# Forgetting attention: the division by the softmax sums moved from the probabilities to the outputs

## The chip, the core and the metric

The kernel runs on one core of a Trainium2 chip. The core has a matrix engine (TensorE, PE in the profile; PEld is its loading of weights), three engines for elementwise work (VectorE or DVE, ScalarE or ACT, GpSimd or POOL), and a queue engine (SyncE, SP) that issues nearly all transfers between memory and the core. Results of TensorE land in eight PSUM banks. The metric is the device time of one execution in microseconds (us); lower is better.

## The reference, cut to what matters

One layer of a streaming encoder on 1024 tokens of width 1024, in float32. A normed input is projected; the columns go to three mixers side by side, whose outputs are joined, projected by `w_o` and added to x; then comes a gated feed-forward part and a last norm. The change lies in the third mixer, forgetting attention, with 8 heads of 64 columns:

```python
s = jnp.einsum('bhqd,bhkd->bhqk', qb, kh) + Fb[..., None] - F[:, :, None, :]
s = jnp.where(kpos[None, :] <= qpos[:, None], s, -jnp.inf)
p = jax.nn.softmax(s, axis=-1)
return jnp.einsum('bhqk,bhkd->bhqd', p, vh)
```

`softmax` divides every row of exponentials by its sum. The division may be done on the exponentials, or after the product with v on the outputs, one divisor for each query and head.

## The kernel before, in words

**Precision.** Every float32 operand of a matmul is split into a high part in a rounded type and the low rest. A product takes three matmuls (high by high, high by low, low by high), in `gemm` (L144) and `woven` (L152).

**Attention.** The 8 heads are worked on as 4 pairs `p` of 2 heads `a` (`fox_attend`, L627). For each head there are four items `m` of two query blocks of 128 (`fox_item`, L549), 32 items in all. An item forms the negated scores `s` of each query block (L575 to L578), adds F and takes the row's minimum on VectorE (L580), and takes the exponential on ScalarE, which also gives the row's sum as a column of `l` (L584). L587 takes reciprocals, and the probabilities are divided in place: the first block by GpSimd (L590), the second by VectorE (L592). Then, in steps of two key blocks, TensorE transposes the probabilities into a bank `pt` (L601), ScalarE and VectorE write the high and low part `pp` (L603, L604), and TensorE multiplies by `v` into the bank `o` (L615). At the end ScalarE copies the lower half of `o` (L618) and VectorE adds the two halves (L621). `o` and `Y` have 64 head columns on the partitions and queries along the free dimension. For pairs 0 to 2 the result is written into a tile `y0` to `y2`, and `keep_mix` (L270) splits it and stores it in memory (`mixs`, L275 and L276). For pair 3 each item writes its part of `last_mix` itself (L624, L625), and that stays on the core.

**What is threaded between.** While pair `p` is worked on, the projections of pair `p+1` (`fox_qk`, L532, tiles `zq`, `zk`; its results are `q`, `k`, `kl`) and, in pairs 0 and 1, of the second half of the values (`fox_values`, `psv`) are on TensorE too. During pairs 2 and 3 it is the output projection. `out_proj` (L651) is called twice for each of the 8 token blocks `tb`: first as `pxa` over the first four groups of mixer columns (L698 to L707), then as `pxb` over the last four. Each call has two groups of 12 matmuls, for two halves of the columns; each group fills a bank of the tag "gm", and L658 adds the bank to the tile `xa` of this token block, which L704 has loaded with x. The tag "gm" has two banks (`BANKS`, L27). `pxb` needs `last_mix` and the weights `wo4` to `wo7`.

**Slots.** Large tiles live in 33 slots of 128 partitions by 1024 elements. A list `idle` of slots is kept while the program is written out:

```python
i = idle.pop(0)                                              # L51, G: take a slot
t_ = big.tile([P, 1024], dtype, tag=f"g{i}", name=name)      # L52
idle.append(where.pop(n))                                    # L58, free: give it back at the end
```

A tile's slot is thus settled by the order in which the program calls `G` and `free`, and the first instruction that writes a tile waits for the last one that uses the tile that had its slot before. Behind pair 2 the program frees the slots of the normed input `hT` (16), of pair 2's `q`, `k`, `kl` and of `v2`, then those of `mh6` and `y2` by `keep_mix`. It then takes, in this order: `mix7` twice, weights `wo0` to `wo3` (two slots each), four mixes, `xa0` to `xa3`, four mixes, `xa4` to `xa7`, and, after giving back the mixes, the weights and pair 3's operands, `wo4` to `wo7`. Other tiles live in rings of a few slots (`RINGS`, L28); the ring `wr`, two slots, holds weights as they come from memory.

**Order.** Each engine works through its own list of instructions in order. These lists are made before the run by a planner (L1119) that follows a simulated time line: an instruction that is ready goes first if it stands earlier in the program, and later work fills the time in which earlier work waits.

Of the kernel before, what the change touches and what calls it, by code (L numbers as in the profile page):

```python
# [9 lines left out]
F32 = mybir.dt.float32  # L10
F32R = mybir.dt.float32r
I8 = mybir.dt.int8
AF = mybir.ActivationFunctionType
ALU = mybir.AluOpType
# [4 lines left out]
P = 128  # L19
# [12 lines left out]
def tile_hybrid_block(ctx: ExitStack, tc, x, w_fv, w_gv, w_zt, w_o, w_gu, w_down, ln, w_pool, w_a3, chans, b_f, consts, out):  # L32
    nc = tc.nc
    ACT, DVE, POOL, PE, SP = nc.scalar, nc.vector, nc.gpsimd, nc.tensor, nc.sync
# [4 lines left out]
    dpool = ctx.enter_context(tc.tile_pool(name="dp", bufs=1, space=bass.MemoryType.DRAM))  # L39
# [10 lines left out]
    def G(name, dtype=F32):  # L50
        i = idle.pop(0)  # L51
        t_ = big.tile([P, 1024], dtype, tag=f"g{i}", name=name)  # L52
        where[name] = i
        return t_

    def free(*names):
        for n in names:
            idle.append(where.pop(n))  # L58

    def R(name, dtype=F32, tag="p"):  # L60

        i = rings[tag].pop(0)
        rings[tag].append(i)
        return big.tile([P, 1024], dtype, tag=f"g{i}", name=name)

    def S(name, cols=1, dtype=F32):
        return sml.tile([P, cols], dtype, tag=f"s{cols}", name=name)

    def f(ap):
        return ap.bitcast(F32)  # L70


    ident = cst.tile([P, P], F32, name="ident")
# [38 lines left out]
    def PS(tag, name):  # L112
        return pst.tile([P, 512], F32, tag=tag, name=name, bufs=BANKS[tag])
# [22 lines left out]
    def half(name, dtype=F32):  # L136
        return rng.tile([P, 512], dtype, tag="tmp", name=name, bufs=2)
# [25 lines left out]
    def names_T(name):  # L163
        return [f"{name}{k}_{c}_{h}" for k in range(4) for c in range(2) for h in range(2)]
# [105 lines left out]
    def keep_mix(k, y):  # L270

        hi = G(f"mh{k}", F32R)
        ACT.activation(hi, y, AF.Copy)
        DVE.tensor_tensor(out=y, in0=y, in1=f(hi), op=ALU.subtract)
        SP.dma_start(mixs[k, :, 0], f(hi))  # L275
        SP.dma_start(mixs[k, :, 1], y)  # L276
        free(f"mh{k}")
# [14 lines left out]
    last_mix = []  # L292
# [253 lines left out]
                    POOL.tensor_copy(t_[a][own[1 - a], csl], f(t_[a][own[a], csl]))  # L546
        return Q, K, KL

    def fox_item(p, a, m, ops, fb, V, Y):  # L549

        Q, K, KL = (t_[a] for t_ in ops)
        nm = f"{p}_{a}_{m}"
        rows = slice(64 * a, 64 * a + 64)
        Pb, Ws = [], []
        l, rl = S(f"l{nm}", 2), S(f"rl{nm}", 2)
        for i in range(2):
            qb = 2 * m + i
            W = P * (qb + 1)
            nh = 1 if W <= 512 else 2
            w = W // nh  # L560
            qs = slice(qb * P, (qb + 1) * P)
            mn = S(f"mn{nm}_{i}")
            if m >= 2:
                pb = R(f"pb{nm}_{i}")
            elif i == 0:
                pb2 = R(f"pb{nm}")
                pb = pb2[:, 0:512]
            else:
                pb = pb2[:, 512:1024]
            top = 3.0e38  # L570
            for h in range(nh):
                s = PS("s", f"s{nm}_{i}_{h}")
                ks = slice(h * w, (h + 1) * w)
                last = h == nh - 1
                PE.matmul(s[:, 0:w], Q[:, qs], K[:, ks], start=True, stop=False)  # L575
                PE.matmul(s[:, 0:w], Q[:, qs], KL[:, ks], start=False, stop=not last)  # L576
                if last:
                    PE.matmul(s[:, w - P:w], identr, maskr, start=False, stop=True)  # L578
                t_ = mn if last else S(f"mw{nm}_{i}")
                DVE.tensor_tensor_reduce(out=pb[:, ks], in0=s[:, 0:w], in1=fb[:, ks], scale=1.0, scalar=top,  # L580
                                         op0=ALU.add, op1=ALU.min, accum_out=t_)
                top = t_[:, 0:1]

            ACT.activation(pb[:, 0:W], pb[:, 0:W], AF.Exp, bias=mn[:, 0:1], scale=-1.0, accum_out=l[:, i:i + 1])  # L584
            Pb.append(pb)
            Ws.append(W)
        DVE.reciprocal(rl, l)  # L587
        for i, (pb, W) in enumerate(zip(Pb, Ws)):
            if i == 0:
                POOL.tensor_tensor(out=pb[:, 0:W], in0=pb[:, 0:W], in1=rl[:, 0:1].broadcast_to([P, W]), op=ALU.mult)  # L590
            else:
                DVE.tensor_scalar(out=pb[:, 0:W], in0=pb[:, 0:W], scalar1=rl[:, 1:2], scalar2=None, op0=ALU.mult)  # L592
        o = PS("o", f"o{nm}")
        for n in range(m + 1):
            pt = PS("pt", f"pt{nm}_{n}")
            pp = R(f"pp{nm}_{n}", F32R, tag="pp")
            cut = P if n == m else 0
            for b in range(2):
                for i in range(b if cut else 0, 2):
                    o0 = 256 * b + P * i - cut * b  # L600
                    PE.transpose(pt[:, o0:o0 + P], Pb[i][:, (2 * n + b) * P:(2 * n + b + 1) * P], ident)  # L601
            w = 512 - cut
            ACT.activation(pp[:, 0:w], pt[:, 0:w], AF.Copy)  # L603
            DVE.tensor_tensor(out=pp[:, 512:512 + w], in0=pt[:, 0:w], in1=f(pp[:, 0:w]), op=ALU.subtract)  # L604
            for b in range(2):
                kb = 2 * n + b
                o0 = cut * b
                v_ = V[p % 2][kb // 4][:, kb % 4, a]
                ph = pp[:, 256 * b:512 - o0] if b else pp[:, 0:256]
                pl = pp[:, 768:1024 - o0] if b else pp[:, 512:768]  # L610
                both = (o[:, o0:256], v_.rearrange("p s e -> p (s e)"), ph)
                high = (o[0:64, o0:256], v_[:, 0], pl)
                last = kb == 2 * m + 1
                for n_, args in enumerate((high, both) if last else (both, high)):
                    PE.matmul(*args, start=(kb == 0 and n_ == 0), stop=(last and n_ == 1))  # L615
        tmp = half(f"ot{nm}")
        ot, oy = tmp[0:64, 0:256], tmp[:, 256:512]
        ACT.activation(ot, o[64:128, 0:256], AF.Copy)  # L618
        if p < 3:
            oy = Y[:, m * 256:(m + 1) * 256]  # L620
        DVE.tensor_tensor(out=oy[rows], in0=o[0:64, 0:256], in1=ot, op=ALU.add)  # L621
        if p == 3:
            hi, lo = (last_mix[m // 2][rows, h, (m % 2) * 256:(m % 2 + 1) * 256] for h in range(2))
            ACT.activation(hi, oy[rows], AF.Copy)  # L624
            POOL.tensor_tensor(out=lo, in0=oy[rows], in1=f(hi), op=ALU.subtract)  # L625

    def fox_attend(p, ops, V, Y):  # L627
        fbs = []
        for a in range(2):
            fb = R(f"fb{p}_{a}", tag="fb")  # L630
            SP.dma_start(fb, Fd[2 * p + a:2 * p + a + 1, :].broadcast_to([P, T]))
            fbs.append(fb)
        for a, m in ([(a, m) for a in range(2) for m in range(4)] if p < 3 else [(a, m) for m in (1, 0, 3, 2) for a in range(2)]):
            fox_item(p, a, m, ops, fbs[a], V, Y)


    x3d = [dpool.tile([P, D], F32, name=f"x3d{tb}") for tb in range(NT)]
# [36 lines left out]
    V = fox_values(0, (B.within(1), o_[0][:1], o_[0][1:], o_[1][:1], o_[1][1:] + B.turned(0), B.turned(1), (), ()))  # L674
    for k in range(8):
        keep_wo(k)
    ops = fox_qk(0)
    free("gv0", "gv1", "attb0", "attb1")
    for p in range(4):
        if p == 3:  # L680
            last_mix += [G(f"mix7_{g}", F32R).rearrange("p (h t) -> p h t", h=2) for g in range(2)]
        Y = G(f"y{p}") if p < 3 else None
        fox_attend(p, ops, V, Y)
        done = [f"{n}{p}_{a}" for n in ("q", "k", "kl") for a in range(2)] + [f"v{p}_{i}" for i in range(2)]
        if p == 1:
            V = fox_values(1)
            free(*[done.pop() for _ in range(2)])
        if p < 3:
            ops = fox_qk(p + 1)
        if p == 2:  # L690
            free(*names_T("hT"))
        if p < 3:
            free(*done)
            keep_mix(4 + p, Y)
            free(f"y{p}")


    ws = [fetch_wo(k) for k in range(4)]  # L698
# [284 lines left out]
    sums = {}  # L983
# [139 lines left out]
```

## Time and profile before

| | us |
|---|---|
| median of 3 runs | 1175.11 |
| lowest and highest | 1174.69, 1177.39 |
| the profiled execution, whole | 1175.42 |
| its span, first to last instruction | 1173.7 |

| stage of the profiled execution | from, to (us) |
|---|---|
| input norm, pooling and linear attention | 0 to 225 |
| forgetting attention, with projections and part of the output projection | 225 to 495 |
| rest of the output projection, second norm | to 541 |
| feed-forward part and last norm | to 1173.7 |

The profile is of one execution, and its times count from the start of the span. A row of a group gives the line, the engine, the operation, the tile that is written and those that are read, the shape, and the count; behind the bar stand the busy time in us and the mean of one instruction in ns, and then the idle time ahead of the group on its engine with what ended it. Tile names have no numbers of heads or blocks, so `y` is every `y0` to `y3`. In a row of one tile or line the three figures are the least, the median and the longest duration in ns. Rows of a timeline begin with the start and the duration in us, and end with the idle time ahead in brackets.

### The profile page before, as it was taken

To read this page: it belongs to the slowest core of one execution; us is meant where nothing else is said; L and a number is where in the kernel's file an instruction comes from. 1 tells how busy PE (TensorE), PEld (TensorE's weight loads), DVE (VectorE), ACT (ScalarE), POOL (GpSimd) and SP (SyncE) were. 2 spreads that over 40 slices of the span, in tenths; PEclk is the share of its full clock that TensorE was granted. 3 is DMA by queue.
4 is the path that set the end of the run, shared out by engine and by line. 5 is a ranking of instruction groups with operands and counts; after the bars stand their busy time and mean duration, and the time that the engine had idled before them with its cause. 6 is when DMAs were issued, how large, how long until landed. Compare 5 with 4: busy or idle time off the path is not lost.

```text
span 1173.7 us, 15953 instructions
## 1 busy us (share of the span) xinstructions
PE 1136.0 (97%) x5928; PEld 958.5 (82%) x5928; DVE 828.2 (71%) x1365; ACT 536.0 (46%) x970; POOL 340.4 (29%) x260
## 2 busy tenths in 40 slices
PE   6999998999999999998999999999999999999996
PEld 5877878889978888886888888888888888888875
DVE  6697364387746866579997767767686685876686
ACT  6454233466654644456453433444344344334345
POOL 2231123343322413210302221022201370660784
PEclk9999999999999999999999999999999999999999
DMA  7121184411203734431323332242314688333233
GB/s 250 37 73 52 59 295 174 176 39 35 91 18 126 305 132 159 173 112 46 117 86 129 101 115 88 101 134 82 135 54 152 224 322 293 103 95 102 86 112 143
DMA packets 57692, 150.45 MB, mean 128 GB/s; under 512 B 5080, under 2 KB 5512, under 8 KB 57616
## 3 DMA queue, kind: packets, MB, share of 16 engines
q1 hardware_dynamic: 57184, 147.87, 36.5%
q0 software_dynamic: 432, 1.57, 0.4%
q8 instruction: 46, 0.75, 0.3%
q14 instruction: 30, 0.25, 0.1%
HBM read 105.09 MB, written 44.34 MB: 127 GB/s over the span
## 4 chain that ended last, share of the span: by engine, by line
PE 76%; DVE 4%; DMA 1%; issue 1%; POOL 1%; ACT 1%; SPq 0%; POOLq 0%; DVEq 0%; ACTq 0%
PE m L774 36%; PE d L1030 15%; PE pxa L144 4%; PE pxb L144 3%; PE o L615 3%; PE pt L601 2%; PE psv L152 2%; PE s L575 1%; PE s L576 1%; PE zq3p L152 1%; PE zq0p L152 1%; PE zq2p L152 1%; PE zk1p L152 1%; PE zk2p L152 1%; PE zk0p L152 1%
## 5 line engine op out<-in xcount | busy, mean ns | idle before, releaser
L774 PE MATMUL m<-hA_0h,wr 128*128 128x512 f32 x616 | 214.7, 391 | 1.2 <-ACT hr L729 1.2
L774 PE MATMUL m<-hA_1h,wr 128*128 128x512 f32 x616 | 214.9, 389 | 0.0
L774 PEld LDWEIGHTS m<-hA_0h,wr 128*128 128x128 f32 x616 | 116.1, 189 | 25.8 <-ACT hr L729 1.6
L774 PEld LDWEIGHTS m<-hA_1h,wr 128*128 128x128 f32 x616 | 115.8, 188 | 24.2
L1030 PE MATMUL d<-lw,ha 128*128 128x512 f32 x308 | 119.9, 389 | 0.9 <-DVE lw L880 0.9
L774 PE MATMUL m<-hA_0l,wr 128*128 128x512 f32 x308 | 120.3, 391 | 0.0
L774 PE MATMUL m<-hA_1l,wr 128*128 128x512 f32 x308 | 119.9, 389 | 0.0
L1030 PE MATMUL d<-hw,ha 128*128 128x512 f32 x308 | 119.3, 389 | 0.0
L1030 PE MATMUL d<-hw,la 128*128 128x512 f32 x308 | 118.4, 389 | 0.0
L756 ACT ACTIVATE wr<-ws 128x512 fp32r<-128x512 f32 x110 | 69.5, 632 | 101.5 <-DVE ws L755 50.1
L826 POOL TENSOR_TENSOR cg<-cu,cu 128x512 f32<-128x512 f32 x11 | 19.7, 1795 | 302.8 <-DVE cu L803 266.7
L757 DVE TENSOR_TENSOR wr<-ws,wr 128x512 fp32r<-128x512 f32 x110 | 76.8, 704 | 20.6 <-ACT wr L756 20.5
L880 DVE TENSOR_TENSOR la<-ra,ha 128x1024 fp32r<-128x1024 f32 (+1 forms) x42 | 57.2, 1368 | 32.0 <-ACT ha L879 24.7
L590 POOL TENSOR_TENSOR pb<-pb,rl 128x128 f32<-128x128 f32 (+3 forms) x32 | 39.0, 1222 | 117.5 <-DVE rl L587 108.9
L872 POOL TENSOR_TENSOR rw<-wd,wd 128x512 f32<-128x512 f32 x33 | 59.0, 1815 | 47.7 <-PE d L1030 47.6
L879 ACT ACTIVATE ha<-ra 128x1024 fp32r<-128x1024 f32 (+1 forms) x42 | 41.3, 987 | 65.6 <-DMA ra<-cd 56.8
L1030 PEld LDWEIGHTS d<-lw,ha 128*128 128x128 f32 x308 | 57.8, 188 | 13.3 <-DVE lw L880 1.3
L604 DVE TENSOR_TENSOR pp<-pt,pp 128x512 fp32r<-128x512 f32 (+1 forms) x80 | 50.2, 631 | 25.7 <-ACT pp L603 25.3
L774 PEld LDWEIGHTS m<-hA_0l,wr 128*128 128x128 f32 x308 | 58.1, 189 | 12.0
L774 PEld LDWEIGHTS m<-hA_1l,wr 128*128 128x128 f32 x308 | 58.0, 188 | 12.0
L1030 PEld LDWEIGHTS d<-hw,la 128*128 128x128 f32 x308 | 57.8, 188 | 12.1
L1030 PEld LDWEIGHTS d<-hw,ha 128*128 128x128 f32 x308 | 57.8, 188 | 11.9
(398 smaller groups left out, 2690.6 us busy)
## 6 DMA issues: line engine op xcount, KB each, us to landing
ra<-cd SPq DMA_DIRECT2D x35, 512.0 KB, 3.9
wu<-in_w_gu_dram SPq DMA_DIRECT2D x22, 512.0 KB, 4.6
wg<-in_w_gu_dram SPq DMA_DIRECT2D x22, 512.0 KB, 3.7
wd<-in_w_down_dram SPq DMA_DIRECT2D x22, 512.0 KB, 6.4
mix<-mixs SPq DMA_DIRECT2D x14, 512.0 KB, 5.3
cd<-cg SPq DMA_DIRECT2D x11, 512.0 KB, 6.3
cd<-cs SPq DMA_DIRECT2D x11, 512.0 KB, 3.4
cd<-cu SPq DMA_DIRECT2D x11, 512.0 KB, 3.3
```

Of the source, the lines that this page charges most:

```text
L144: PE.matmul(ps, a, b, start=(n == 0), stop=(n == last))
L152: PE.matmul(ps, a, b, start=(i == 0 and n == 0), stop=(i == len(terms) - 1 and n == 2))
L590: POOL.tensor_tensor(out=pb[:, 0:W], in0=pb[:, 0:W], in1=rl[:, 0:1].broadcast_to([P, W]), op=ALU.mult)
L604: DVE.tensor_tensor(out=pp[:, 512:512 + w], in0=pt[:, 0:w], in1=f(pp[:, 0:w]), op=ALU.subtract)
L615: PE.matmul(*args, start=(kb == 0 and n_ == 0), stop=(last and n_ == 1))
L756: ACT.activation(hi, src, AF.Copy)
L757: DVE.tensor_tensor(out=lo, in0=src, in1=f(hi), op=ALU.subtract)
L774: PE.matmul(ps, a, b, start=(n == 0), stop=(n == 11))
L872: POOL.tensor_tensor(out=raw_[:, j * 512:j * 512 + 512], in0=wd[h0, j0 + j][:, e0, :], in1=wd[h1, j0 + j][:, e1, :], op=op)
L879: ACT.activation(hi[:, sl], src, AF.Copy)
L880: DVE.tensor_tensor(out=lo[:, sl], in0=src, in1=f(hi[:, sl]), op=ALU.subtract)
L1030: PE.matmul(banks[t], a[:, o], b[:, ns], start=(j0 + j == 0 and m == 0), stop=(j0 + j == NF // 2 - 1 and m == 2))
```

## The change

The probabilities stay undivided: `fox_item` no longer has L587 to L592, and the row sums of a pair go into one tile `sums` of 16 columns. A new function `divide(p, Y, sums, g)` handles half `g` of the queries (512) for both heads of a pair. It takes the reciprocals of 8 columns of sums (VectorE), transposes them to 8 rows (TensorE, ScalarE), stores these in memory (`Ld`), loads them back in two transfers, one for each head, each spread over 64 partitions, and multiplies `Y` (VectorE, 128x512). `rt` and `rb`, the turned and the spread divisors, share a slot of the ring `wr`. For pairs 0 to 2 it is called behind the next pair's projections and ahead of `keep_mix`. Pair 3 now has a tile `y3` in a slot of its own, taken behind `mix7` and given back at the end of its attention; `divide(3, 0)` stands behind the fourth item, `divide(3, 1)` behind the last, and it writes the high and low part of `last_mix` (ScalarE, VectorE).

```diff
@@ -546,13 +546,12 @@
                     POOL.tensor_copy(t_[a][own[1 - a], csl], f(t_[a][own[a], csl]))
         return Q, K, KL
 
-    def fox_item(p, a, m, ops, fb, V, Y):
+    def fox_item(p, a, m, ops, fb, V, Y, sums):
 
         Q, K, KL = (t_[a] for t_ in ops)
         nm = f"{p}_{a}_{m}"
         rows = slice(64 * a, 64 * a + 64)
-        Pb, Ws = [], []
-        l, rl = S(f"l{nm}", 2), S(f"rl{nm}", 2)
+        Pb = []
         for i in range(2):
             qb = 2 * m + i
             W = P * (qb + 1)
@@ -581,15 +580,8 @@
                                          op0=ALU.add, op1=ALU.min, accum_out=t_)
                 top = t_[:, 0:1]
 
-            ACT.activation(pb[:, 0:W], pb[:, 0:W], AF.Exp, bias=mn[:, 0:1], scale=-1.0, accum_out=l[:, i:i + 1])
+            ACT.activation(pb[:, 0:W], pb[:, 0:W], AF.Exp, bias=mn[:, 0:1], scale=-1.0, accum_out=sums[:, col(a, qb)])
             Pb.append(pb)
-            Ws.append(W)
-        DVE.reciprocal(rl, l)
-        for i, (pb, W) in enumerate(zip(Pb, Ws)):
-            if i == 0:
-                POOL.tensor_tensor(out=pb[:, 0:W], in0=pb[:, 0:W], in1=rl[:, 0:1].broadcast_to([P, W]), op=ALU.mult)
-            else:
-                DVE.tensor_scalar(out=pb[:, 0:W], in0=pb[:, 0:W], scalar1=rl[:, 1:2], scalar2=None, op0=ALU.mult)
         o = PS("o", f"o{nm}")
         for n in range(m + 1):
             pt = PS("pt", f"pt{nm}_{n}")
@@ -613,16 +605,33 @@
                 last = kb == 2 * m + 1
                 for n_, args in enumerate((high, both) if last else (both, high)):
                     PE.matmul(*args, start=(kb == 0 and n_ == 0), stop=(last and n_ == 1))
-        tmp = half(f"ot{nm}")
-        ot, oy = tmp[0:64, 0:256], tmp[:, 256:512]
+        ot = half(f"ot{nm}")[0:64, 0:256]
         ACT.activation(ot, o[64:128, 0:256], AF.Copy)
-        if p < 3:
-            oy = Y[:, m * 256:(m + 1) * 256]
-        DVE.tensor_tensor(out=oy[rows], in0=o[0:64, 0:256], in1=ot, op=ALU.add)
+        DVE.tensor_tensor(out=Y[rows, m * 256:(m + 1) * 256], in0=o[0:64, 0:256], in1=ot, op=ALU.add)
+
+
+    Ld = dpool.tile([4, 2, 2, 512], F32, name="Ld")
+
+    def col(a, qb):
+        c = 8 * (qb // 4) + 4 * a + qb % 4
+        return slice(c, c + 1)
+
+    def divide(p, Y, sums, g):
+
+        nm = f"{p}_{g}"
+        rw = R(f"rb{nm}", tag="wr")
+        rl, rt, rb, gs = S(f"rl{nm}", 8), rw[0:8, 512:640], rw[:, 0:512], slice(g * 512, g * 512 + 512)
+        DVE.reciprocal(rl, sums[:, 8 * g:8 * g + 8])
+        pt = PS("pt", f"ptl{nm}")
+        PE.transpose(pt[0:8, 0:P], rl, ident)
+        ACT.activation(rt, pt[0:8, 0:P], AF.Copy)
+        SP.dma_start(Ld[p, g].rearrange("a (q t) -> (a q) t", t=P), rt)
+        for a in range(2):
+            SP.dma_start(rb[64 * a:64 * a + 64, :], Ld[p, g, a:a + 1, :].broadcast_to([64, 512]))
+        DVE.tensor_tensor(out=Y[:, gs], in0=Y[:, gs], in1=rb, op=ALU.mult)
         if p == 3:
-            hi, lo = (last_mix[m // 2][rows, h, (m % 2) * 256:(m % 2 + 1) * 256] for h in range(2))
-            ACT.activation(hi, oy[rows], AF.Copy)
-            POOL.tensor_tensor(out=lo, in0=oy[rows], in1=f(hi), op=ALU.subtract)
+            ACT.activation(last_mix[g][:, 0], Y[:, gs], AF.Copy)
+            DVE.tensor_tensor(out=last_mix[g][:, 1], in0=Y[:, gs], in1=f(last_mix[g][:, 0]), op=ALU.subtract)
 
     def fox_attend(p, ops, V, Y):
         fbs = []
@@ -630,8 +639,14 @@
             fb = R(f"fb{p}_{a}", tag="fb")
             SP.dma_start(fb, Fd[2 * p + a:2 * p + a + 1, :].broadcast_to([P, T]))
             fbs.append(fb)
+        sums = S(f"l{p}", 16)
         for a, m in ([(a, m) for a in range(2) for m in range(4)] if p < 3 else [(a, m) for m in (1, 0, 3, 2) for a in range(2)]):
-            fox_item(p, a, m, ops, fbs[a], V, Y)
+            fox_item(p, a, m, ops, fbs[a], V, Y, sums)
+            if p == 3 and (a, m) == (1, 0):
+                divide(p, Y, sums, 0)
+        if p == 3:
+            divide(p, Y, sums, 1)
+        return sums
 
 
     x3d = [dpool.tile([P, D], F32, name=f"x3d{tb}") for tb in range(NT)]
@@ -679,8 +694,8 @@
     for p in range(4):
         if p == 3:
             last_mix += [G(f"mix7_{g}", F32R).rearrange("p (h t) -> p h t", h=2) for g in range(2)]
-        Y = G(f"y{p}") if p < 3 else None
-        fox_attend(p, ops, V, Y)
+        Y = G(f"y{p}")
+        sums = fox_attend(p, ops, V, Y)
         done = [f"{n}{p}_{a}" for n in ("q", "k", "kl") for a in range(2)] + [f"v{p}_{i}" for i in range(2)]
         if p == 1:
             V = fox_values(1)
@@ -691,8 +706,10 @@
             free(*names_T("hT"))
         if p < 3:
             free(*done)
+            for g in range(2):
+                divide(p, Y, sums, g)
             keep_mix(4 + p, Y)
-            free(f"y{p}")
+        free(f"y{p}")
 
 
     ws = [fetch_wo(k) for k in range(4)]
```

## The prediction

> **What bounds the kernel now.** I read the page's first part, then the busy time by stretches of the attention stage, TensorE's waits there, and the chain that ended last.
>
> ```profile
> span 1173.7 us, 15953 instructions
> PE 1136.0 (97%) x5928; PEld 958.5 (82%) x5928; DVE 828.2 (71%) x1365; ACT 536.0 (46%) x970; POOL 340.4 (29%) x260
> ```
>
> TensorE is the bound by far, and the change takes no matrix product away. So the question is whether TensorE keeps its cover in the stage that the change touches. The next view is busy time in two stretches of the stage (columns: stretch, its length, then PE, PEld, DVE, ACT and POOL busy with instruction counts, granted clock, DMA share, GB/s), then two of the five rows of TensorE's waits between 225 and 500 us.
>
> ```profile
> 345.00:390.00 45.00, 41.76 (x232) 35.64 (x231) 31.01 (x69) 22.53 (x50) 14.79 (x17) 0.96 0.44 159
> 465.00:500.00 35.00, 34.78 (x199) 29.65 (x198) 19.88 (x33) 16.03 (x36) 8.08 (x12) 1.00 0.48 175
> ```
>
> ```profile
> PE zq3p L152 <- DVE kl L544: 2.5, 1, 2.5
> PE pxb L144 <- DMA wo6h<-wod: 0.2, 1, 0.2
> ```
>
> Attention leaves TensorE almost no hole, because projections and the output projection are threaded between its steps. There is one real stall, 2.5 us, where pair 1 ends and the next projection waits for `kl`; it also pulls the clock to 0.96 over 45 us, (1 - 0.96) x 45 = 1.8 us more. What division costs in the kernel before:
>
> ```profile
> L587 DVE RECIPROCAL rl<-l x32: 145/166/169, 231.7 to 466.4; 128x2 f32<-128x2 f32 x32
> L592 DVE TENSOR_SCALAR pb<-pb,rl x32: 333/732/2273, 231.9 to 466.6; 128x256 f32<-128x256 f32 x8, 128x512 f32<-128x512 f32 x8, 128x768 f32<-128x768 f32 x8, 128x1024 f32<-128x1024 f32 x8
> L590 POOL TENSOR_TENSOR pb<-pb,rl x32: 401/1160/2517, 232.4 to 466.8; 128x128 f32<-128x128 f32 x8, 128x384 f32<-128x384 f32 x8, 128x640 f32<-128x640 f32 x8, 128x896 f32<-128x896 f32 x8
> ```
>
> **What is removed.** 32 x 0.73 = 23 us of VectorE and 32 x 1.16 = 37 us of GpSimd (by the medians), 24 of 32 reciprocals, and in each of 32 items the latency of the longer of two scalings, 1 us or so, between exponential and transpose. None of it is on TensorE's path while other matmuls fill in. It can only come back at the one place where they run out, the 2.5 us stall at the end of pair 1 with its 1.8 us of clock: bounds 0 and -4.3 us, and the two holes of 0.34 us ahead of it that are shown below under (a), together 0 to -5. I take -2.5, the middle, since what TensorE waits for there hangs on the last items of pair 1, and earlier items help only if the planner then leaves projections over to cover them.
>
> **What is added.** Eight divisions. Each is a transposed reciprocal, a copy, a store, two spreading loads, and one or three operations on 128x512.
>
> ```profile
> L235 PE MATMUL pa<-ident,g x8: 271/272/273, 24.7 to 56.0; 128*8 128x128 f32 x8
> L901 DVE TENSOR_TENSOR hs<-hr,hr 128x512 f32<-128x512 f32 x16 | 10.3, 679 | 0.0
> L756 ACT ACTIVATE wr<-ws 128x512 fp32r<-128x512 f32 x110 | 69.5, 632 | 101.5 <-DVE ws L755 50.1 <-DMA cd<-cs 18.2 <-PE m L774 14.5
> L757 DVE TENSOR_TENSOR wr<-ws,wr 128x512 fp32r<-128x512 f32 x110 | 76.8, 704 | 20.6 <-ACT wr L756 20.5
> ```
>
> TensorE gains eight transposes of the very form of L235: at most 8 x 0.27 = 2.2 us, less where they overlap neighbours, at least 0.5; I take +1. VectorE's 8 x 0.68 us is below the 23 us removed. SP issues 24 DMAs more, 0.32 us each as in the rows of L275 below, on a queue that mostly waits. For pairs 0 to 2 the result goes to memory and is read late, so it costs nothing; the cover is the following pair's attention. If that cover is gone, `y0`'s slot holds up `k2_1` and `y1`'s holds up `kl3_1`, the last user of each being the store of `keep_mix`.
>
> **What is moved: the slot list.** This decides the matter. `G` takes the first name of a first-in, first-out list, and a tile waits for the last user of the one that had its slot. I followed the list. Before pair 3 it holds, in order, fifteen slots of `hT`, then those of q2_0, q2_1, k2_0, k2_1, kl2_0, kl2_1, v2_0, v2_1, `mh6` and `y2`. Before the change, mix7 takes two, `wo0` to `wo3` eight, the first mixes four, xa0 the last `hT`, xa1 to xa3 the next three, the second mixes four, and then xa4 = v2_1, xa5 = `mh6`, xa6 = `y2`, xa7 = a mix slot. The trace agrees: two of the four late loads of `xa` wait for just these stores.
>
> ```profile
> SPq L704 <- DMA mixs<-mh: 2.5, 1, 2.5
> SPq L704 <- DMA mixs<-y: 1.6, 1, 1.6
> ```
>
> ```profile
> 436.42 0.32 SPq L275 DMA_DIRECT2D mixs<-mh  x1
> 438.17 0.32 SPq L276 DMA_DIRECT2D mixs<-y  x1
> 441.05 2.35 SPq L704 DMA_DIRECT2D xa<-in_x_dram  x2
> 466.08 0.33 SPq L289 DMA_DIRECT2D wo5l<-wod  x1
> ```
>
> After the change `y3` takes one slot more behind mix7, and gives it back at the end of the list, behind `y2`. All later tiles move up one: xa4 = `mh6`, xa5 = `y2`, and **xa6 = `y3`**. So the load of x for token block 6 waits until the last instruction on `y3`, the subtraction that ends `divide(3, 1)`: the end of all attention. Who waits for xa6: the additions of L658. These empty the "gm" banks, of which there are two, used in turn by pxa6, pxa7 and then all of pxb. Behind the load on SP's queue stand those of wo5l to wo7h, which wait for pxa7 anyway. Before, these additions ran well ahead of the end of attention (VectorE's timeline, then the last item's ACT and DVE steps):
>
> ```profile
> 456.42 0.69 DVE L658 TENSOR_TENSOR xa<-pxa,xa 128x512 f32<-128x512 f32 x1 [2.06 <-PE pxa L144]
> 468.26 0.69 DVE L658 TENSOR_TENSOR xa<-pxa,xa 128x512 f32<-128x512 f32 x1 [1.05 <-PE pxa L144]
> ```
>
> ```profile
> 492.95 0.38 ACT L618 ACTIVATE ot<-o 64x256 f32<-64x256 f32 x1 [3.34 <-PE o L615]
> 493.37 0.42 DVE L621 TENSOR_TENSOR ot<-o,ot 64x256 f32<-64x256 f32 x1 [0.85 <-ACT ot L618]
> ```
>
> pxa6 was added at 456.4 and pxa7 finished at 468.3, while attention ended at 493. From there on the cover of attention was pxa7 and a third of pxb. After the change that cover cannot start before attention is over, and the loss has four terms.
>
> (a) Attention's rest without cover. These rows are busy time on tile o, then on tile pt, after 460.4 us (PE, PEld, DVE, ACT); then ACT and TensorE where pair 1 ends, the one place where attention already runs without filler.
>
> ```profile
> 460.40:493.10 32.70, 8.51 (x56) 7.48 (x56) 1.25 (x3) 1.29 (x4) 1.00 0.40 145
> 460.40:493.10 32.70, 5.58 (x37) 4.26 (x37) 6.94 (x11) 6.05 (x11) 1.00 0.40 145
> ```
>
> ```profile
> 345.76 1.09 ACT L603 ACTIVATE pp<-pt 128x512 fp32r<-128x512 f32 x2
> 348.30 1.17 ACT L603 ACTIVATE pp<-pt 128x512 fp32r<-128x512 f32 x2 [1.45 <-PE pt L601]
> ```
>
> ```profile
> 347.14 0.68 PE L615 MATMUL o<-pp,v 128*64 128x256 f32 x4 [0.34 <-DVE pp L604]
> 349.67 0.98 PE L615 MATMUL o<-pp,v 128*64 128x256 f32 x7 [0.34 <-DVE pp L604]
> ```
>
> Eleven steps are left. Uncovered, two take 348.30 - 345.76 = 2.54 us (349.67 - 347.14 = 2.53 on TensorE), so eleven take 14.0 us, against 8.5 + 5.6 = 14.1 us of busy time on TensorE. By these rows nothing is lost beyond one hole of 0.34 us for two steps, 5.5 x 0.34 = 1.9 us. Busy time counts the ends of matmuls that overlap the next one's start, so the hole may be twice that: 0 to +4, and I take +1.5.
>
> (b) From the last o to the first matmul of pxa7: ot 0.38, sum 0.42, product 0.68, copy 0.63, difference 0.70, and five hand-overs of 0.04 us (493.37 - 492.95 - 0.38), 3.0 us together; the load of xa6; the addition 0.69.
>
> ```profile
> DMA to landing us min/median/max: 3.3/6.0/10.3
> ```
>
> I take 4.0 for that load, near the minimum, because few transfers run beside it: 3.0 + 4.0 + 0.7 = 7.7 us. Part of the 5.5 us of pxa6 itself (24 matmuls, as in the row of pxb below) can still lie there if attention is ahead of its old pace; half of it leaves +5. Bounds: 7.7 - 5.5 = 2.2, and with the median load 9.7.
>
> (c) wo5l to wo7h sit in slots that pxa7's last group frees, before and after the change. Two pieces of the chain that ended last:
>
> ```profile
> 467.00 7.58 DMA wo6h<-wod
> 498.34 5.50 PE pxb L144 x24
> ```
>
> The wait for wo6h stands in the chain already; attention filled it. With attention over, nothing does: from the issue of wo6h TensorE has about six matmuls of pxa7 and twelve of pxb at 5.50 / 24 = 0.23 us, 4.1 us, then idles about 7.6 - 4.1 = 3.5 us, and about 1 more until the other loads land, +4.5 (3 to 7).
>
> (d) Clock. The stall at 353 us cost 1.8 us in granted clock, worked out above. Terms (b) and (c) are two such stalls, 2 us each, +4 (2 to 6). [...]
>
> Sum: -2.5 + 1 + 1.5 + 5 + 4.5 + 4 = +13.5 us on the profiled execution's 1175.4 us (its span and 1.7 us around it), 1188.9 us; that execution lies 0.3 us above the median of the runs shown, so I leave the sum as it is. The ends of the terms give -5 + 0.5 + 0 + 2.2 + 3 + 2 = +2.7, and 0 + 2.2 + 4 + 9.7 + 7 + 6 = +28.9.
>
> The load of `divide`, from memory to 128 rows, has a row of its own kind:
>
> ```profile
> fb<-Fd SPq DMA_DIRECT2D x8, 512.0 KB, 4.3
> ```
>
> A store and a load after it are thus some 6 to 8 us. VectorE's product waits for them in order, and behind it are queued the next pp differences and the xa additions. The last exponentials come more than that before the last o, so I price it at nothing; this is a rival too.
>
> **Rivals.** *Faster (0.10).* Attention, 1 us of latency shorter in each of 32 items, ends before pxa6 is due. Then xa6 is no brake, (a) and (b) vanish, and the stall at pair 1 goes: -5 + 1 = -4, 1171.4 us. It decides if `y3` is done about 8 us before pxa6's addition, that is attention ends by 448 instead of 493; for it speaks only that TensorE is never idle there, against it that 45 us are needed and 32 are all the latency removed. *No change (0.08).* Gains at pair 1 cancel a small (c), 1175 us. [...] *Slower by another way (0.10).* The product of `divide` stands too early in VectorE's order and holds it for the 6 us of its loads, in eight places, 2 us of it uncovered each time: 16 + 1 - 2.5 = +14.5, near 1190 us, with the losses spread over all four pairs instead of after 460 us.
>
> **From this the numbers.** My forecast has 0.72. A measurement of this kernel tells about 0.3%, 3.5 us. Slower by more: 0.72 + 0.10 = 0.82; within: 0.08; faster: 0.10. The range runs from 1176, just below the lower end of the sum (1178.1), to 1204, its upper end (1204.3); faster and part of no change lie outside.
>
> **What would show it.** Right: no L590 and L592; L704 waiting tens of us for a DVE of `mix`; the pxa7 and pxb matmuls all behind the last ot; a hole of 5 to 8 us in TensorE around the end of attention, one of 3 to 5 us soon after it that ends on a wo load, a clock below 1.00 in that stretch; the stages from there on shifted but equal. Wrong: pxa7 additions before the last ot (the slot theory falls), TensorE idle in pairs 0 to 2 with VectorE waiting for the spreading loads, or a hole that ends on something else than xa6.

## The result, and the profile after

| | before | after |
|---|---|---|
| median (us) | 1175.95 of 4 runs | 1217.63 of 4 runs |
| lowest and highest (us) | 1174.69, 1177.39 | 1214.29, 1218.20 |
| span of the profiled execution (us) | 1173.7 | 1215.4 |

After to before is 1.035, with an interval from 1.0329 to 1.0371: the change costs 41.7 us where 13.5 were forecast. One run of experiment a below, the profiled one, was disturbed (2937.17 us) and is left out, so a has no trace to read. The page's first lines of the changed kernel:

```profile
span 1215.4 us, 15883 instructions
PE 1147.7 (94%) x5936; PEld 965.0 (79%) x5936; DVE 811.7 (67%) x1319; ACT 533.0 (44%) x972; POOL 295.4 (24%) x220
```

GpSimd lost 45 us of work and VectorE 16.5, yet the span grew: TensorE went from 97% to 94% of a longer span. Busy time by four stretches says where, for the kernel before (columns as in the prediction: stretch, length, PE, PEld, DVE, ACT, POOL, clock, DMA share, GB/s):

```profile
225.00:300.00 75.00, 75.00 (x513) 69.56 (x512) 54.91 (x144) 46.59 (x101) 27.21 (x26) 1.00 0.11 36
300.00:465.00 165.00, 161.27 (x943) 140.11 (x942) 112.03 (x267) 85.15 (x182) 48.27 (x44) 0.99 0.41 142
465.00:545.00 80.00, 75.10 (x391) 62.76 (x390) 57.44 (x84) 45.48 (x98) 14.69 (x22) 0.98 0.34 123
545.00:620.00 75.00, 75.00 (x332) 62.05 (x332) 73.16 (x114) 36.74 (x63) 13.38 (x8) 1.00 0.32 101
```

And for the changed kernel:

```profile
225.00:300.00 75.00, 70.19 (x422) 61.06 (x422) 50.97 (x140) 52.36 (x113) 13.88 (x15) 0.96 0.18 60
300.00:465.00 165.00, 158.33 (x972) 141.25 (x971) 84.24 (x207) 75.16 (x166) 19.68 (x21) 0.99 0.38 133
465.00:545.00 80.00, 59.56 (x299) 48.08 (x298) 33.11 (x55) 21.65 (x48) 3.99 (x9) 0.89 0.35 119
545.00:620.00 75.00, 68.70 (x312) 56.29 (x311) 67.33 (x103) 43.47 (x83) 8.65 (x9) 0.95 0.18 64
```

TensorE's idle time in the four stretches was 0, 3.7, 4.9 and 0 us, 8.6 together, and is now 4.8, 6.7, 20.4 and 6.3, 38.2 together: 29.6 us more. The clock that was not granted, (1 - clock) x length, was 3.3 us and is 17.2: 13.9 more. The two sums overlap, since the clock stood at 0.50 from 491.9 to 501.9 us, where TensorE did nothing, but together they are the size of the loss. Half of it stands around the end of attention, at 487 us, and a part stands where nothing was forecast, in the end of pair 0 before 300 us. TensorE's waits in the changed kernel from 225 to 620 us, by what ended them (line numbers in a row are those of the kernel that ran, so L673 here is L658 in the kernel before):

```profile
PE pxa L144 <- DVE xa L673: 15.0, 1, 15.0
...
PE pt L593 <- DVE pp L596: 8.3, 6, 3.4
...
PE pxb L144 <- DMA wo6h<-wod: 2.5, 1, 2.5
...
PE pxb L144 <- DMA wo5l<-wod: 1.0, 1, 1.0
```

The first is the slot of the forecast: one hole of 15.0 us, at the first matmul of pxa7, waiting for an addition to xa6. The last two are the wo loads of term (c). The second is new. The stall at the end of pair 1, `zq3p` behind `kl`, is gone; in the same list `zq2p` and `zk2p` now wait 1.4 and 1.2 us. The chain through the hole is read from three timelines, first VectorE's:

```profile
476.20 0.20 DVE L624 RECIPROCAL rl<-l 128x8 f32<-128x8 f32 x1 [0.61 <-ACT pb L583]
...
487.39 0.42 DVE L610 TENSOR_TENSOR y<-o,ot 64x256 f32<-64x256 f32 x1 [0.41 <-ACT ot L609]
...
494.29 0.69 DVE L631 TENSOR_TENSOR y<-y,rb 128x512 f32<-128x512 f32 x1 [6.48 <-DMA rb<-Ld]
...
501.21 1.29 DVE L673 TENSOR_TENSOR xa<-pxa,xa 128x512 f32<-128x512 f32 x2 [4.84 <-DMA xa<-in_x_dram]
```

Then TensorE's and SP's:

```profile
486.15 0.27 PE L626 MATMUL ptl<-ident,rl 128*8 128x128 f32 x1
486.18 0.76 PE L607 MATMUL o<-pp,v 128*128 128x256 f32 x4
501.95 0.79 PE L144 MATMUL pxa<-wo0h,mix 128*128 128x512 f32 x1 [15.01 <-DVE xa L673]
```

```profile
486.75 0.30 SPq L628 DMA_DIRECT2D Ld<-rb  x1
...
488.39 1.11 SPq L630 DMA_DIRECT2D rb<-Ld  x2
...
496.40 0.33 SPq L721 DMA_DIRECT2D xa<-in_x_dram  x1
```

The divisors' reciprocal was ready at 476.4, and the product with `y3` could have stood right behind the last output, at 487.8. But the transpose that turns the divisors ran only at 486.15, among the last matmuls of attention, and from there the way through memory took until 494.29. So 6.48 us of the 15.0 are VectorE's wait for the divisors, and 4.84 its wait for xa6.

### The profile page after: what moved, and what is told of

It is laid out like the page before. It is cut to its first block, busy times and chain, and to the rows that moved or that the text cites. A ratio compares the mean times of both kernels' runs of the same rounds, so it can differ in the third digit from the quotient of the medians.

```text
span 1215.4 us, 15883 instructions
## 1 busy us (share of the span) xinstructions
PE 1147.7 (94%) x5936; PEld 965.0 (79%) x5936; DVE 811.7 (67%) x1319; ACT 533.0 (44%) x972; POOL 295.4 (24%) x220
## 5 line engine op out<-in xcount | busy, mean ns | idle before, releaser
L897 DVE TENSOR_TENSOR la<-ra,ha 128x1024 fp32r<-128x1024 f32 (+1 forms) x42 | 59.9, 1433 | 31.3 <-ACT ha L896 24.0
L897 DVE TENSOR_TENSOR lw<-rw,hw 128x1024 fp32r<-128x1024 f32 (+1 forms) x30 | 51.4, 1725 | 13.7 <-ACT hw L896 13.4
```

The lines of the kernel that those rows point to most:

```text
L897: DVE.tensor_tensor(out=lo[:, sl], in0=src, in1=f(hi[:, sl]), op=ALU.subtract)
```

## The experiments

**Theories.** The first: the slot list makes x for token block 6 wait for the end of `divide(3, 1)`, and this is most of the loss, in pair 3 alone. The rival: `divide` itself costs, in every pair, by holding VectorE for the loads of its divisors. A third possibility is that probabilities left undivided change the order to the worse. Every edit is against the changed kernel unless said otherwise; times are medians, and each ratio is to the kernel before on the same chip. The median of that kernel was 1175.95 us beside the changed kernel, 1175.64 beside a to d, 1177.26 beside e to h and 1176.49 beside i, k and l, so a difference between two runs of different groups is uncertain by about as much as these differ.

**a: only pair 3 changed.** Pairs 0 to 2 divide the probabilities as before.

```diff
+        if not (p == 3):
+            DVE.reciprocal(rl, l)
...
-            for g in range(2):
-                divide(p, Y, sums, g)
```

> Only pair 3 divides outputs (with y3 in its slot); pairs 0 to 2 divide probabilities as before. Slot theory (the load of xa6 waits for y3, and the end of attention loses its cover): nearly all of the loss after 475 us stays, +26 to +32, so 1202 to 1208 us. Rival (the spreading loads hold VectorE, alike in all eight divisions): two eighths of +42, about 1186 us.

1207.29 us (three runs), ratio 1.0272 (1.0246 to 1.0297), +31.7 us.

**b: only pairs 0 to 2 changed.** Pair 3 as before: no `y3`, no `divide` there.

```diff
-        Y = G(f"y{p}")
+        Y = G(f"y{p}") if p < 3 else None
...
-            if p == 3 and (a, m) == (1, 0):
-                divide(p, Y, sums, 0)
-        if p == 3:
-            divide(p, Y, sums, 1)
```

> Only pairs 0 to 2 divide outputs; pair 3 as before, without y3. Slot theory: the end of attention is as before, and what is left is what the trace after shows between 250 and 475 us, +7 to +13, so 1183 to 1189 us; the loads of the weights wfv_0 and wfv_1 still come late, at 288 us or so. Rival (loads hold VectorE alike everywhere): six eighths of +42, about 1207 us.

1183.67 us, ratio 1.0076 (1.0047 to 1.0104), +8.0 us. Pair 3 and the other pairs add up: 31.7 + 8.0 = 39.7 of 41.7. So three quarters of the loss are pair 3's, and pairs 0 to 2 are not free, as I had them.

**c: no division at all.** This kernel leaves out the division by the sums, and pair 3 is written as before. It shows the removal by itself.

```diff
-            for g in range(2):
-                divide(p, Y, sums, g)
...
-        Y = G(f"y{p}")
+        Y = G(f"y{p}") if p < 3 else None
```

> No division at all: probabilities are left undivided and outputs are not divided either, pair 3 written as before. This is the gain of the removal alone. My account: the stall at the end of pair 1 goes, -5 to 0, so 1171 to 1176 us, since TensorE is the bound. Rival (the scalings were on the path): -10 or more, 1166 us or less.

1175.5 us, ratio 0.9995 (0.9981 to 1.0009): removing all scalings gains nothing that can be measured (at most 0.19%, 2.2 us, by the interval). The page of c has 31.1 us less of VectorE and 40.6 less of GpSimd than in the kernel before, and TensorE's waits still have the stall of pair 1, a hair longer than before:

```profile
PE 1135.7 (97%) x5928; PEld 959.7 (82%) x5928; DVE 797.1 (68%) x1301; ACT 534.3 (45%) x970; POOL 299.8 (26%) x228
```

```profile
PE zq3p L152 <- DVE kl L544: 2.6, 1, 2.6
```

So my gain of 2.5 us is not there, and undivided probabilities do not harm either. The stall's disappearance in the changed kernel has another cause (g).

**d: `y3` out of the slot list.** It takes a tile of the ring "w" instead; all divisions stay.

```diff
-        Y = G(f"y{p}")
+        Y = G(f"y{p}") if p < 3 else R("y3", tag="w")
```

> As the changed kernel, but y3 takes a slot of the ring w (idle by then) and none of the list, so xa4 to xa7 have the slots that they had before. Slot theory: the 15 us hole and what follows it go, 1184 to 1192 us, and pxa7 and a part of pxb stand before the last item's end again. Rival (the round trip of the divisors through memory is what costs): 1208 us or more.

1189.29 us, ratio 1.0117 (1.0089 to 1.0146), +13.6 us. One line gives back 28.3 us (1217.63 - 1189.29). The 15 us hole is gone; TensorE's two stretches behind pair 2 in d:

```profile
465.00:545.00 80.00, 76.33 (x405) 63.06 (x403) 53.46 (x82) 40.81 (x87) 7.65 (x15) 1.00 0.40 140
545.00:620.00 75.00, 69.72 (x302) 57.43 (x303) 73.46 (x115) 38.09 (x69) 11.20 (x7) 0.95 0.28 93
```

Between 465 and 545 us TensorE is busier than in the kernel before, 76.3 to 75.1.

**e: the slot alone.** The kernel before, with the probabilities divided in every item, and `y3` added as a tile of the slot list; at the places of `divide(3, g)` only the split into `last_mix` is left. No divisor goes through memory. The split thus comes later than in the kernel before, where each item makes its own, and e prices the slot and this delay together.

```diff
-        Y = G(f"y{p}") if p < 3 else None
+        Y = G(f"y{p}")
...
-            free(f"y{p}")
+        free(f"y{p}")
```

> The kernel before (all probabilities divided), but pair 3's outputs go through y3 in its slot of the list and are split into last_mix at the end, 512 queries at a time; no divisors in memory. Slot theory: the load of xa6 still waits for the end of attention, without the 7.5 us of the round trip in front of it, so +18 to +26, 1194 to 1202 us, and the hole in TensorE is 7 to 9 us instead of 15. Rival (the round trip makes the loss of pair 3): +5 or less.

1201.91 us, ratio 1.0209 (1.0194 to 1.0224), +24.7 us. A tile more in the list, with no division moved, costs more than I gave the whole change. TensorE's timeline in e, and two rows of its waits:

```profile
476.19 1.90 PE L617 MATMUL o<-pp,v 128*128 128x256 f32 x12
486.67 0.80 PE L144 MATMUL pxa<-wo0h,mix 128*128 128x512 f32 x1 [8.58 <-DVE xa L672]
```

```profile
PE pxa L144 <- DVE xa L672: 10.7, 2, 8.6
...
PE pxb L144 <- DMA wo6h<-wod: 3.2, 1, 3.2
```

Between the last product with v and the first matmul of pxa7 TensorE idles 8.6 us. My chain has 7.7, less 0.7 for a product that e does not make, 7.0 without cover. Half of pxa6, which I had lying there as cover, does not: 168 matmuls of `pxa`, seven blocks of 24, stand ahead of the last o in e and in the changed kernel.

**f: the turn of pair 3's divisors in another bank.** The transpose takes a bank of the tag "s" instead of "pt", in both divisions of pair 3.

```diff
-        pt = PS("pt", f"ptl{nm}")
+        pt = PS("s" if p == 3 else "pt", f"ptl{nm}")
```

> As the changed kernel, but pair 3's reciprocals are turned in a bank of the tag s, whose last user is the last score, not of the tag pt, whose last user is the last transpose. If the round trip came after attention only because the bank was taken in program order, it moves under the last items: the hole falls from 15 to 7 to 9 us, and the time by 6 to 8 us to 1209 to 1212 us. Rival (the planner would put the transpose last in any bank): no change, 1215 us or more.

1208.61 us, ratio 1.0264 (1.0244 to 1.0284), +31.4 us: 9.0 us less than the changed kernel, or 10.3 by the two losses (41.7 - 31.4). TensorE's timeline, SP's and VectorE's in f:

```profile
474.59 0.27 PE L626 MATMUL ptl<-ident,rl 128*8 128x128 f32 x1
...
483.53 1.90 PE L607 MATMUL o<-pp,v 128*128 128x256 f32 x12
494.62 0.80 PE L144 MATMUL pxa<-wo0h,mix 128*128 128x512 f32 x1 [9.19 <-DVE xa L673]
```

```profile
475.98 0.30 SPq L628 DMA_DIRECT2D Ld<-rb  x1
477.21 1.12 SPq L630 DMA_DIRECT2D rb<-Ld  x2
```

```profile
486.33 0.69 DVE L631 TENSOR_TENSOR y<-y,rb 128x512 f32<-128x512 f32 x1
```

The turn (the transpose of the divisors) now runs 9 us before the last group of products with v, VectorE's product no longer waits for the loads, and the hole shrinks from 15.0 to 9.2 us, close to e's. In the changed kernel the turn thus waited for its bank: banks of a tag are taken in the order of the program, and `divide(3, 1)` is written behind the last item's transposes, which use the same tag. The cover that I counted on was there; the order of the bank kept the round trip from using it. Not all of f's 9.0 us is shown to be the bank's, though: the hole is 5.8 us shorter, and 3.0 us (0.04 x 75) lie from 225 to 300 us, where the changed kernel was granted a clock of 0.96 and f one of 1.00, while the edit touches pair 3 alone.

**g: the next weights ahead of `divide`.** The loads of the value weights (pair 0) and of pair 3's projection weights (pair 1) are written ahead of the divisions, since both use the ring `wr`.

```diff
+            if p == 0:
+                early["fv"] = load_fv(1)
+            if p == 1:
+                early.update({f"z{n}3": load_w(w_zt[:, 6 + i, :], f"z{n}3", eng=POOL) for i, n in enumerate("qk")})
             for g in range(2):
                 divide(p, Y, sums, g)
```

> As the changed kernel, but the weights of the next stage (wfv for the second half of the values, zq3 and zk3) take their slots of the ring wr ahead of divide(0) and divide(1). Ring theory: the uncovered end of pair 0 (250 to 300 us) gets its filler psv back, -7 to -11 us, 1206 to 1211 us. Rival (VectorE waiting for the spreading loads is what costs there): still 1215 us or more.

1211.0 us, ratio 1.0289 (1.0274 to 1.0304), +33.7 us: 6.6 us less than the changed kernel, or 8.0 by the two losses (41.7 - 33.7). SP's timeline, of the kernel before, of the changed one and of g:

```profile
218.84 0.33 SPq L117 DMA_DIRECT2D wfv_0r<-in_w_fv_dram  x1
```

```profile
286.95 1.09 SPq L630 DMA_DIRECT2D rb<-Ld  x2
288.22 0.45 SPq L117 DMA_DIRECT2D wfv_0r<-in_w_fv_dram  x1
```

```profile
219.50 0.33 SPq L117 DMA_DIRECT2D wfv_0r<-in_w_fv_dram  x1
```

In the changed kernel these weights waited 69 us for pair 0's two divisions, which stood ahead of them in the ring's two slots. The matmuls of `psv` that they feed are the cover of pair 0's end; without it TensorE idles (4.8 us before 300 us, 0 in g), and the late `psv` (its last matmul starts at 337.2 us, in the kernel before at 310.5) then covers the end of pair 1, where it is not due. With g the cover is back in place, and with it the old stall of 2.5 us. TensorE's first stretch in g:

```profile
225.00:300.00 75.00, 75.00 (x511) 69.40 (x510) 44.03 (x125) 46.10 (x103) 14.37 (x15) 1.00 0.09 27
```

**h: the spread by TensorE, `y3` in the ring.** No way through memory: each row of divisors is spread over 64 partitions by a product with a column of the identity repeated 64 times, into a bank that VectorE multiplies from.

```diff
+        rb = PS("s", f"rb{nm}")
+        for q in range(4):
+            for a in range(2):
+                c = 4 * a + q
+                PE.matmul(rb[64 * a:64 * a + 64, q * P:(q + 1) * P], ident[0:8, c:c + 1].broadcast_to([8, 64]), rt,
+                          start=True, stop=True)
```

> Outputs divided in all pairs, y3 in a slot of the ring w, and no memory in it: the turned reciprocals are spread by eight small matmuls (a column of the identity, repeated, by the 8x128 reciprocals) into a bank, which VectorE multiplies from. No ring wr, no transfer. If slot, ring and round trip are the whole loss: 1174 to 1179 us, the added 72 small matmuls costing 1 to 3 us. Rival (dividing late costs in itself, by VectorE's order): 1185 us or more.

1202.31 us, ratio 1.0216 (1.02 to 1.0231), +25 us: the expectation fell. One part is plain from TensorE's timeline of h: each product was issued as two matmuls, and the sixteen of one division take 1.09 us, so up to 8.7 us in eight divisions. Another part is that `pxb` waits for mixes:

```profile
521.07 1.09 PE L629 MATMUL rb<-rt,ident 8*64 8x128 f32 x16
...
525.54 0.80 PE L144 MATMUL pxb<-wo4h,mix 128*128 128x512 f32 x1 [2.79 <-DMA mix<-mixs]
```

Attention's last product with v is issued at 519.7 us in h, 33.5 later than in the changed kernel: the planner put 96 matmuls of `pxb` ahead of it. The kernel before has 66 ahead, and issues its last product at 492.6.

**i: d and g together.** `y3` is in the ring "w", and the next weights stand ahead of `divide`.

> The changed kernel with y3 in a slot of the ring w and the weights of the next stage ahead of divide(0) and divide(1) in the ring wr. If slot and ring are separate losses, their measured shares (28.3 us and 6.6 us) add: 1180 to 1185 us. Rival (what the ring costs is won back by the end of pair 1 as soon as the end of attention is covered): no better than 1189 us.

1181.84 us, ratio 1.0045 (1.0029 to 1.0061), +5.3 us, as expected: the two repairs take away 35.8 of the 41.7 us, nearly the sum of each alone (28.3 + 6.6 = 34.9).

**l: i, with the product on GpSimd.**

```diff
-        DVE.tensor_tensor(out=Y[:, gs], in0=Y[:, gs], in1=rb, op=ALU.mult)
+        POOL.tensor_tensor(out=Y[:, gs], in0=Y[:, gs], in1=rb, op=ALU.mult)
```

> As i_weights_first_y3_ring, but the product of outputs and spread divisors is done by GpSimd, which waits for the loads in VectorE's place. If what is left there is VectorE held by the spreading loads: 1175 to 1180 us. Rival (the rest is of another kind): as i_weights_first_y3_ring within 2 us.

1179.51 us, ratio 1.0018 (1.0007 to 1.0029), +3.0 us. In the changed kernel VectorE stands waiting for the spreading loads; in l GpSimd does, 71 us in six places, and has little else to do (46.2 us of work in the 275 from 225 to 500). One row of VectorE's waits in the changed kernel, from 225 to 500 us:

```profile
DVE y L631 <- DMA rb<-Ld: 21.3, 7, 6.6
```

In i, with ring and slot mended, this wait is 14.8 us in seven places. Taking it and the product from VectorE is worth 2.3 us of time, if anything: i's runs go from 1180.27 to 1186.05 and l's from 1177.15 to 1181.18, so the medians stand apart and the ranges overlap.

**k: the spread by transposes, `y3` in the ring.** GpSimd repeats each column of divisors 64 times, and four transposes turn them straight into a bank; half of each division moves up between the items.

```diff
+        POOL.tensor_copy(rr.rearrange("p (q a e) -> p q a e", q=4, a=2),
+                         rl.rearrange("p (a q o) -> p q a o", a=2, o=1).broadcast_to([P, 4, 2, 64]))
+        rb = PS("pt", f"rb{nm}")
+        for q in range(4):
+            PE.transpose(rb[:, q * P:(q + 1) * P], rr[:, q * P:(q + 1) * P], ident)
```

> Outputs divided in all pairs without memory: GpSimd repeats the reciprocals along the free dimension, four transposes of 128x128 turn and spread them at once in a bank of the tag pt, VectorE multiplies from there; half 0 is divided as soon as its items are done, y3 is in the ring w, the ring wr is not used. If dividing late costs nothing in itself: the 1175.5 us without any division and 32 transposes of 0.11 us, 1177 to 1181 us. Rival (the banks and VectorE's order make it dear in any form, as with the spreading by matmuls): 1190 us or more.

1198.31 us, ratio 1.0169 (1.015 to 1.0187), +21.8 us: the expectation fell, and the time is one that the rival gave. No divisor goes through memory here, and TensorE has 32 short transposes in place of eight; yet by their losses it is 8.2 us slower than d (21.8 - 13.6), which keeps the way through memory. The last product with v is issued at 511.2 us, again with 96 matmuls of `pxb` ahead of it, and TensorE waits for mixes in k as in h:

```profile
PE pxb L144 <- DMA mix<-mixs: 5.1, 2, 3.2
```

Why the planner ends attention later in h and k, I can only argue: a bank of "s" or "pt" is held by the spread divisors until the outputs are there to be multiplied, which slows the items, and the mixes that `pxb` needs wait for slots that the end of attention frees. No run isolates this, and it stays open.

## Why the prediction was right about the slot and wrong about the loss

**The slot, terms (a) to (d).** Right as a mechanism: xa6 waits for `y3`, pxa7 and all of `pxb` stand behind the last o, and two wo loads follow. e prices it, with the later split, at +24.7 us, where the four terms gave 1.5 + 5 + 4.5 + 4 = 15. In e's trace additions to `xa` hold TensorE for 10.7 us in two places, where (b) had 5; the two wo loads take 4.4 us (3.2 and 1.2), where (c) had 4.5; and `pt` waits 2.8 us for `pp`, where (a) had 1.5. The other 6.8 us are left to the clock, (d), and to a longer wait in the second norm; no run divides them.

**The step that failed: (b), +5, and the sentence that priced the divisors' way through memory at nothing.** I argued that the last exponentials come long before the last o, and they do: the reciprocal is ready at 476.4, ten us ahead. But I looked only at when the data is ready. The transpose takes a bank of "pt" behind those of the last item, so it ran 9.75 us after the reciprocal was ready (486.15 - 476.4), and of the round trip from 486.15 to 494.29 the last 6.48 us lay bare. The 6 to 8 us that I put on a store and a load were right (486.75 to 494.29 is 7.5); the cover was wrong. f, which moves only that bank, shortens the hole by 5.8 us. The other part of the error in (b) is the cover by pxa6, which e shows to be none: its hole is 8.6 where I had 5. The load of xa6, taken at 4.0, took 4.8 (496.40 to 501.21). The hole is thus 15.0 in place of 5.

**(a), +1.5.** Behind 475 us the four short waits of `pt` and `o` for `pp` are 1.7 us together in the changed kernel, so the size was about right.

**(c), +4.5.** TensorE waited 2.5 us for wo6h and 1.0 for wo5l in the rows above, 3.5 together; 4.5 with bounds of 3 to 7 holds.

**(d), +4 for the clock.** The windows give 13.9 us more of clock not granted from 225 to 620 us, which counts time in which TensorE stood still. Asked in narrow stretches, the trace of the changed kernel shows half the clock (0.50 or 0.51) from 294.0 to 300.8, 454.4 to 457.8, 491.9 to 505.6, 515.8 to 519.3 and 577.3 to 584.1 us, that of the kernel before from 353.7 to 357.1 and 541.5 to 544.9. Of the third stretch only the end, from 501.95 on, lies behind the hole; with the fourth, behind the wait for wo6h, that is 7.1 us at half the clock, 3.5 us, near my 4. The first two, at the ends of pairs 0 and 2, I had not counted: 10.2 us at half the clock, 5.1 us. The end of the third shows in the rows: behind the 15 us hole eight matmuls start every 0.43 us and the later ones every 0.23:

```profile
502.97 0.63 PE L144 MATMUL pxa<-wo0h,mix 128*128 128x512 f32 x1
503.40 0.63 PE L144 MATMUL pxa<-wo1h,mix 128*128 128x512 f32 x1
...
506.50 0.39 PE L144 MATMUL pxa<-wo0h,mix 128*128 128x512 f32 x1
506.73 0.39 PE L144 MATMUL pxa<-wo0l,mix 128*128 128x512 f32 x1
```

That is 8 x 0.2 = 1.6 us for one hole, near the 2 us that I took for each and the 1.8 of the 2.5 us stall in the kernel before: a hole of 15 us did not have a higher price than one of 2.5. I was short in the number of holes, not in the price of one.

**The removal, -2.5.** Wrong. c takes away every scaling and stays at 0.9995, with the stall of pair 1 in place. The pages say why: TensorE is busy for 97% of the span before and in c, and 40.6 us of GpSimd and 31.1 of VectorE were worth nothing that c can show. The forecast sign "the stall goes" came true for another reason, the displaced `psv`.

**Pairs 0 to 2, nothing.** Wrong by 8.0 us (run b). I looked at the slots of `y0` and `y1` and at SP's queue, and missed the ring `wr`: its two slots are the two divisions' own, and the next weights stand behind them. g prices that at 6.6. One of my signs of being wrong was TensorE idle in pairs 0 to 2 with VectorE waiting for the spreading loads, and it came. At the end of pair 2 VectorE waits for them, the split of `y` for `keep_mix` follows late, and TensorE waits for the `pp` behind it (VectorE's timeline, then TensorE's):

```profile
446.79 0.69 DVE L631 TENSOR_TENSOR y<-y,rb 128x512 f32<-128x512 f32 x1 [2.79 <-DMA rb<-Ld]
...
450.70 1.23 DVE L274 TENSOR_TENSOR y<-y,mh 128x1024 f32<-128x1024 f32 x1 [1.54 <-ACT mh L273]
```

```profile
452.58 0.55 PE L593 MATMUL pt<-ident,pb 128*128 128x128 f32 x3 [3.36 <-DVE pp L596]
```

**The rival "slower by another way", +14.5 by VectorE held for the loads.** The wait is there, 21.3 us in seven places, and a part of it reaches TensorE, as at 452.58 us. With ring and slot mended, 14.8 us of it are left, and taking them off VectorE gives 2.3 us (l against i), so its 16 us were too many.

**Sum.** With the terms that the runs give: 24.7 for the slot (e), 9.0 for the turn behind the last transposes (f), 6.6 for the ring (g) and 2.3 for VectorE's wait (l against i) make 42.6 beside 41.7 measured. That the two meet so closely is luck. The terms come from different kernels and overlap: 24.7 and 9.0 are more than all of pair 3 in a, 31.7, and than the 28.3 that d gives back, and a part of f's 9.0 lies at the end of pair 0. The firmer account is i and l: slot and ring together are 35.8 us, VectorE's wait about 2.3, and in l 3.0 us of the change are still there (0.18%, below what I called the measurement's 0.3%, though its interval, 1.0007 to 1.0029, stays above 1); what they are stays open. TensorE's wait for the second norm's squares (`n2pt`), 5.7 us here and 3.5 before, does not make the loss by itself: c has 5.8 at the time of the kernel before, l has 3.8.

Of the signs that I named for being right, some came (pxa7 and all of pxb behind the last `ot`, a clock below 1.00) and some did not: the hole was 15.0 us where I had 5 to 8, the waits for wo loads 2.5 and 1.0 where I had one of 3 to 5, and SP did not stand tens of us at the load of x. It stood 12 us at the store of the divisors ahead of it, which waits for the turn's copy. SP's queue, worked through in order, showed its first wait here, not the one that mattered.

## What to carry to other kernels

Where slots, banks and ring places are handed out in program order, price an edit by walking each of those lists past it, not by its instructions: here one tile more in a list cost 24.7 us (e), a transpose in the wrong bank up to 9.0 (f), and a small tile in a shared ring 6.6 (g). When a transfer is said to be hidden, check the order of every resource that its first step takes, and not only when its data is ready. Work removed from engines that are not the bound (72 us in c) gained nothing here, so it could not pay for even one new wait of the engine that is.

## What the runs showed of the hardware that was not expected

The way of a 4 KB tile through memory into two halves of 64 rows took 7.5 us from the store to VectorE's use (486.75 to 494.29), with two other transfers issued between the store and the loads. A float32 product of 8 rows by 128 columns was issued as two matmuls, sixteen for one division in 1.09 us, where the way through memory needs one transpose of 0.27 us on TensorE; by their losses h is 11.4 us slower than d (25.0 - 13.6), though not for this alone. Behind a stop of 15 us TensorE lost 1.6 us to the clock, no more than the 1.8 read for one of 2.5 us in the kernel before. The clock was at 0.50 for 3.4 us from 353.7 us in the kernel before and from 454.4 us in the changed kernel, where TensorE was at work again, behind waits of 2.55 and 3.36 us, since 353.19 and 452.58 us: of a stretch of the same length ahead, it was busy for 0.85 us in the first and for 1.76 in the second.
